# Feed-forward by seven products: product order, one more pair in part two's down projection, and left-side sums kept in DRAM

## The chip, the cores and the metric

The kernel runs on one core of one Trainium2 chip. The metric is the device time of one execution in microseconds (us); the median of several runs counts.

## What is computed

One layer of a decoder block on 256 tokens of width 2048, all in float32:

```
h = h + 1/2 * SwiGLU_a(RMSNorm(h))          # gate/up 2048 -> 2 x 5632, down 5632 -> 2048
h = h + mixer(RMSNorm(h))                    # one input projection, DeltaNet + stick-breaking, one output projection
h = h + 1/2 * SwiGLU_b(RMSNorm(h))
h = h + sigmoid(RMSNorm(h) @ W_pg) * (p @ W_pp)
out = RMSNorm(h)
swiglu(x) = (silu(x @ w_gate) * (x @ w_up)) @ w_down
```

The change touches the two SwiGLU feed-forwards alone.

## The kernel before

**Numbers.** Each float32 matrix is split into a high and a low part (fp32r), and a product takes three matmuls: high by high, high by low, low by high. Weights come from HBM as pairs: 256 rows by 512 columns, 512 KB, by `weight_pair` (L71 the load on SyncE's queue into one of four `raw` buffers, L74 the high part on ScalarE, L75 the low part on VectorE). A plain pair is 12 matmuls of 512 columns: 2 halves of the rows, 2 halves of the tokens, 3 matmuls each (L540 to L542 in the feed-forward). `next_weights` hands out the pairs in the order of one list and prepares up to two ahead.

**Groups.** A feed-forward (`ffn`) is a chain of groups of four PSUM banks (2 token halves by 2 column blocks). `PARTS` cuts the 11 blocks of the hidden width into part one (blocks 0 to 2), part two (3 to 6) and part three (7 to 10). Each part is one gate/up group ("gu") per block and then two down groups ("dn", column blocks 0 and 1, then 2 and 3) that contract over the part's blocks alone. A part of four blocks has eight pairs in its down projection, a part of three has six.

**Seven products.** Of each group the first `ns` pairs are not multiplied plainly. Over a pair, the two token halves, the two halves of the 256 rows and the two column blocks form a 2 by 2 by 2 block product, and the Winograd form needs seven products instead of eight: per pair 7 x 3 = 21 matmuls in place of 2 x 12 = 24. `NS` is 4 for gu groups and `NS_DOWN` is (2, 3, 3) for the down groups of the parts. Weight quarters of the `ns` pairs lie in four tiles R (L276, GpSimd's queue, `ns` x 256 KB each, named (0,0), (0,1), (1,1), (1,0)); `all_sums` makes the seven weight sides from them: VectorE sums (L304), accumulating DMAs on GpSimd's queue that add a quarter from HBM onto a tile (L311, `add_loaded`), and for each product a high part (L295, ScalarE) and a low part (L296, VectorE) in one of two buffers. The first three products take the running sums in (0,0), the fourth takes (0,1) after an accumulating DMA, the fifth takes (1,0) as loaded, the sixth (1,1), the seventh (0,0) after another accumulating DMA. `product` runs the matmuls (L339 to L341): first and second into banks c21 and c12, third and fourth into c21, fifth into c11, sixth into c12, seventh into c21. After the first two the result is copied to c11 and c22 (L344, ScalarE); after the third and the fourth c21 is copied out (L347, ScalarE) and subtracted from c12 or c22 (L349, VectorE). So the fourth product, which adds onto c21, waits for the copy of c21 after the third.

**Where the products stand.** A group's seven products are issued while the group before it does its plain pairs, one after each pair from the second or third pair on (`plan`). If the plain pairs run out, the rest follows the last one. The loads of R for the group after next are placed behind the fifth, sixth and seventh product and behind the next group's first plain pair, into the tiles in the order in which they come free (`loads`).

**Left sides.** Products one, five and seven take the left factor as it is; the other four take sums and differences of its quarters, made by `halves` in a lane beside the matmuls (L452 a sum, four L458, L460 high part on ScalarE, L461 low part on VectorE) into the tiles Sh and Sl. There is one pair of these tiles. They hold the normed input's sums ("gu"), then the hidden blocks' sums ("dn"), then the normed input's again: `halves("gu")` runs at the start of a feed-forward and again when the second down group of parts one and two begins (L518).

**The hidden blocks.** After a gu group `down_input` multiplies by the gate (L477), transposes on VectorE (L482), writes to DRAM (L488), reads back (L493, both on SyncE's queue for a part's last block) and splits (L499 ScalarE, L500 VectorE). The pairs of a part's last block come last in the first down group. `last` (L573) is the number of lane steps between the read and the split.

The order on each engine is set when the program is built: a scheduler takes the instructions in about the order of the source, but moves them past each other by what it expects to be ready; `keep_in_program_order` stops it from that for one instruction.

## Time and profile before

| | |
|---|---|
| median of 3 runs | 1952.89 us (1952.71 to 1953.48) |
| the profiled execution | 1953.25 us, of it 1951.5 us from the first to the last instruction |
| granted TensorE clock, mean | 0.998 |
| TensorE busy | 1932.7 us (99%), 8884 matmuls |
| VectorE busy | 1567.9 us (80%) |
| ScalarE busy | 1163.1 us (60%) |
| DMA | 475.06 MB, 243 GB/s over the span |

A share of the span is an average over stages. Matmuls are pipelined: each row shows some 389 ns, while the next one starts some 227 ns later, so time is read from start to start, and an idle time shown before a matmul leaves out the last one's tail (about 0.16 us).

### The profile page before, as it was taken

What the parts mean: (1) busy time and instruction counts of PE and PEld (TensorE: products, weight loads), DVE (VectorE), ACT (ScalarE), POOL (GpSimd) and SP (SyncE); (2) the same over time, 40 slices, a digit from 0 to 9 for tenths busy, and PEclk for the clock granted to TensorE, in tenths of its full rate; (3) what the DMA queues carried; (4) which work ended last, traced back from release to release, by engine and by line L of the source; (5) the groups of instructions that cost most, each with busy time, mean ns of one, the idle gap of its engine ahead of it and who ended that gap; (6) DMA issues with size and microseconds to landing.
All of it is one profiled execution on the core that took longest, in us unless ns stands there. A gap on an engine that the chain in (4) does not pass through costs nothing.

```text
span 1951.5 us, 24163 instructions
## 1 busy us (share of the span) xinstructions
PE 1932.7 (99%) x8884; PEld 1591.6 (82%) x8884; DVE 1567.9 (80%) x1679; ACT 1163.1 (60%) x1358; POOL 148.8 (8%) x226
## 2 busy tenths in 40 slices
PE   9999999999999999999999999999999999999997
PEld 7888888888888888878788888888888788887886
DVE  7889878997889766797856579889888987888965
ACT  6656666566665567664555456566565755656653
POOL 0010100000010000010100000010000100001000
PEclk9999999999999999999999999999999999999999
DMA  8778888788887765556565786888898987988864
GB/s 311 268 238 276 255 288 285 227 293 251 282 283 237 225 216 172 175 169 209 173 201 160 244 289 226 226 285 289 241 282 251 303 266 237 272 255 282 249 208 141
DMA packets 144184, 475.06 MB, mean 243 GB/s; under 512 B 19649, under 2 KB 47297, under 8 KB 129857
## 3 DMA queue, kind: packets, MB, share of 16 engines
q1 hardware_dynamic: 107200, 302.16, 44.4%
q0 software_dynamic: 25920, 160.44, 30.2%
q10 hardware_dynamic: 10944, 10.91, 1.7%
q8 instruction: 69, 1.13, 0.2%
q14 instruction: 51, 0.41, 0.1%
HBM read 451.44 MB, written 22.02 MB: 243 GB/s over the span
## 4 chain that ended last, share of the span: by engine, by line
PE 87%; DVE 6%; DMA 4%; issue 2%; ACT 1%; SPq 0%; POOL 0%; POOLq 0%; DVEq 0%; ACTq 0%
PE g L340 5%; PE d L541 5%; PE d L542 5%; PE g L339 5%; PE d L540 4%; PE g L341 4%; PE u L540 4%; PE u L542 4%; PE u L541 4%; PE g L541 4%; PE g L542 4%; PE pj L109 4%; PE pj L110 4%; PE pj L111 4%; PE g L540 4%
## 5 line engine op out<-in xcount | busy, mean ns | idle before, releaser
L74 ACT CAST whi<-raw 128x1024 fp32r<-128x1024 f32 (+1 forms) x489 | 512.1, 1050 | 427.1 <-PE pj L111 109.9
L75 DVE TENSOR_TENSOR wlo<-raw,whi 128x1024 fp32r<-128x1024 f32 (+1 forms) x489 | 592.0, 1217 | 166.1 <-ACT whi L74 163.8
L296 DVE TENSOR_TENSOR slo<-R,shi 128x2048 fp32r<-128x2048 f32 (+2 forms) x224 | 445.2, 1989 | 149.0 <-ACT shi L295 147.6
L295 ACT CAST shi<-R 128x2048 fp32r<-128x2048 f32 (+2 forms) x224 | 374.2, 1671 | 140.5 <-DVE R L304 62.1
L109 PE MATMUL pj<-whi,nTh 128*128 128x512 f32 x448 | 179.4, 401 | 0.0
L110 PE MATMUL pj<-wlo,nTh 128*128 128x512 f32 x448 | 175.3, 391 | 1.1 <-DVE wlo L75 1.1
L111 PE MATMUL pj<-whi,nTl 128*128 128x512 f32 x448 | 174.9, 390 | 0.0
L541 PE MATMUL d<-wlo,hTh 128*128 128x512 f32 x448 | 174.3, 389 | 0.0
L540 PE MATMUL d<-whi,hTh 128*128 128x512 f32 x448 | 174.2, 389 | 0.0
L542 PE MATMUL d<-whi,hTl 128*128 128x512 f32 x448 | 173.7, 389 | 0.0
L541 PE MATMUL g<-wlo,nTh 128*128 128x512 f32 x400 | 155.9, 390 | 0.4 <-DVE wlo L75 0.4
L541 PE MATMUL u<-wlo,nTh 128*128 128x512 f32 x400 | 155.7, 389 | 0.5 <-DVE wlo L75 0.5
L542 PE MATMUL g<-whi,nTl 128*128 128x512 f32 x400 | 155.8, 390 | 0.0
L542 PE MATMUL u<-whi,nTl 128*128 128x512 f32 x400 | 155.7, 389 | 0.0
L540 PE MATMUL g<-whi,nTh 128*128 128x512 f32 x400 | 155.4, 390 | 0.0
L540 PE MATMUL u<-whi,nTh 128*128 128x512 f32 x400 | 154.2, 389 | 0.2 <-ACT whi L74 0.2
L304 DVE TENSOR_TENSOR R<-R 128x2048 f32<-128x2048 f32 (+2 forms) x68 | 135.7, 1995 | 0.1
L110 PEld LDWEIGHTS pj<-wlo,nTh 128*128 128x128 f32 x448 | 84.2, 188 | 18.9 <-DVE wlo L75 2.7
L111 PEld LDWEIGHTS pj<-whi,nTl 128*128 128x128 f32 x448 | 84.1, 188 | 17.6
L542 PEld LDWEIGHTS d<-whi,hTl 128*128 128x128 f32 x448 | 84.1, 188 | 17.6
L541 PEld LDWEIGHTS d<-wlo,hTh 128*128 128x128 f32 x448 | 84.1, 188 | 17.6
L540 PEld LDWEIGHTS d<-whi,hTh 128*128 128x128 f32 x448 | 84.1, 188 | 17.4
(332 smaller groups left out, 3445.2 us busy)
## 6 DMA issues: line engine op xcount, KB each, us to landing
raw<-in_w_gu SPq DMA_DIRECT2D x199, 512.0 KB, 5.7
raw<-in_w_down SPq DMA_DIRECT2D x112, 512.0 KB, 6.5
raw<-in_w_in SPq DMA_DIRECT2D x112, 512.0 KB, 3.4
R<-in_w_gu2q POOLq DMA_DIRECT2D x54, 1024.0 KB, 8.6
R<-in_w_gu1q POOLq DMA_DIRECT2D x48, 1024.0 KB, 8.6
raw<-in_w_out SPq DMA_DIRECT2D x32, 512.0 KB, 4.2
tT<-scr SPq DMA_DIRECT2D x22, 512.0 KB, 5.1
R<-in_w_down11q POOLq DMA_DIRECT2D x12, 768.0 KB, 6.0
```

What stands on the lines that cost most here:

```text
L74: nc.scalar.copy(hi[:, j, :], raw[:, j, :])
L75: nc.vector.tensor_tensor(out=lo[:, j, :], in0=raw[:, j, :], in1=hi[:, j, :], op=ALU.subtract)
L109: nc.tensor.matmul(outs[t], xh[:, c], whi[:, j, :], start=st, stop=False)
L110: nc.tensor.matmul(outs[t], xh[:, c], wlo[:, j, :], start=False, stop=False)
L111: nc.tensor.matmul(outs[t], xl[:, c], whi[:, j, :], start=False, stop=sp)
L295: keep(nc.scalar.copy(hi, w))
L296: nc.vector.tensor_tensor(out=lo, in0=w, in1=hi, op=ALU.subtract)
L304: keep(nc.vector.tensor_tensor(out=self.raw[x], in0=self.raw[x], in1=self.raw[y], op=ALU.add))
L339: nc.tensor.matmul(out, xh, whi[:, g, :], start=st, stop=False, skip_group_check=True)
L540: nc.tensor.matmul(out, xh[:, c], whi[:, j, :], start=st, stop=False, skip_group_check=True)
L541: nc.tensor.matmul(out, xh[:, c], wlo[:, j, :], start=False, stop=False, skip_group_check=True)
L542: nc.tensor.matmul(out, xl[:, c], whi[:, j, :], start=False, stop=sp, skip_group_check=True)
```

## The change

Three things. The fifth product is put in front of the fourth (`SEVEN`), with its weight side, and the order in which the R tiles are taken over follows. The two down groups of part two take four pairs by seven products instead of three, so their plain pairs go from ten to eight each, and their left sides get a fourth pair. The sums of the normed input's left sides are written to DRAM once, sixteen lane steps after they are made, and read back into Sh and Sl in eight DMAs of 256 KB on SyncE's queue, at the second lane step of the second down group of parts one and two, instead of being computed again. The tiles Sh and Sl are laid out with the quarter outermost, and in part two `last` goes from 3 to 2.

```diff
@@ -28,7 +28,10 @@
 
 
 NS = 4
-NS_DOWN = tuple(3 if i1 - i0 == 4 else 2 for i0, i1 in PARTS)
+NS_DOWN = (2, 4, 3)
+
+
+SEVEN = (0, 1, 2, 4, 3, 5, 6)
 
 
 W_IN_ORDER = (2, 0, 4, 3, 1, 5, 8, 10, 12, 9, 11, 13, 6, 7)
@@ -278,7 +281,7 @@
         def loads(self, last=None):
 
 
-            free = [last.home[q] for q in ((0, 1), (1, 0), (1, 1), (0, 0))] if last else ["R0", "R1", "R2", "R3"]
+            free = [last.home[q] for q in ((1, 0), (0, 1), (1, 1), (0, 0))] if last else ["R0", "R1", "R2", "R3"]
             self.queue = nc.gpsimd if last else nc.sync
             use = (0, 0), (0, 1), (1, 1), (1, 0)
             self.home = dict(zip(use, free))
@@ -310,8 +313,8 @@
                     return add(x, y)
                 nc.gpsimd.dma_start(out=self.raw[x], in_=self.quarters[y[1]][y[0]], accum_op=ALU.add)
 
-            for i, q in enumerate(((0, 0), (0, 0), (0, 0), (0, 1), (1, 0), (1, 1), (0, 0))):
-                ws = halved(*q)
+            for i in SEVEN:
+                ws = halved(*((0, 0), (0, 0), (0, 0), (0, 1), (1, 0), (1, 1), (0, 0))[i])
                 if i == 0:
                     add((0, 0), (0, 1))
                     add_loaded((0, 1), (1, 1))
@@ -417,49 +420,69 @@
     order += [("pair", a["w_pg"][2][g]) for g in range(KD // 2)] + [("pair", a["w_pp"][2])]
     order.append(("pair", a["w_pp"][3]))
 
-    def halves(kind, his, los, ns, wait=0):
-
-
-        for _ in range(wait):
-            yield
-        fp = current[0]
-
-        sh = fp.tile([P, NS, 2, 2, P], F32R, tag="Sh", name="Sh")
-        sl = fp.tile([P, NS, 2, 2, P], F32R, tag="Sl", name="Sl")
+    def new_sides(kind, his, los):
+
+        sh, sl = [current[0].tile([P, 4, NS, P], F32R, tag=x, name=x) for x in ("Sh", "Sl")]
 
         def side(i, g):
             if i in (0, 4, 6):
                 k, t = 2 * (g % 2) + (i > 0), i // 6
                 c = slice(t * P, (t + 1) * P)
                 return his[g // 2][:, k, c], los[g // 2][:, k, c]
-            j, t = {1: (1, 1), 2: (0, 0), 3: (0, 1), 5: (1, 0)}[i]
-            return sh[:, g, j, t, :], sl[:, g, j, t, :]
+            jt = {1: 3, 2: 0, 3: 1, 5: 2}[i]
+            return sh[:, jt, g, :], sl[:, jt, g, :]
 
         sides[kind] = side
-
-        for g0 in range(0, ns, 2):
-            n = min(2, ns - g0)
-            hi, lo = his[g0 // 2], los[g0 // 2]
+        return sh, sl
+
+    def kept_sides(his, los, copy):
+
+        yield
+        both = new_sides("gu", his, los)
+        for jt in (3, 0, 1, 2):
+            for i in range(2):
+                nc.sync.dma_start(out=both[i][:, jt].bitcast(F32), in_=copy[:, i, jt])
+
+    def halves(kind, his, los, ns, wait=0, copy=None):
+
+
+        for _ in range(wait):
+            yield
+        fp = current[0]
+
+        both = new_sides(kind, his, los)
+        for g0, n in {1: ((0, 1),), 2: ((0, 2),), 3: ((0, 2), (2, 1)),
+                      4: ((0, 2), (2, 1), (3, 1)) if kind == "dn" else ((0, 2), (2, 2))}[ns]:
+            k0 = 2 * (g0 % 2)
+            hi, lo = (x[g0 // 2][:, k0:k0 + 2 * n] for x in (his, los))
             keep = lambda ins: ins
-            if g0 and n == 1:
+            if g0 >= 2 and n == 1:
 
                 keep = tc.keep_in_program_order
-                yield
+                if g0 == 2:
+                    yield
             if n == 2:
                 x = fp.tile([P, 2 * NB], F32, tag="sil", name="S")
             else:
                 x = act.tile([P, NB], F32, tag="nat", name="S", bufs=4)
-            keep(nc.vector.tensor_tensor(out=x, in0=hi[:, 0:2 * n].bitcast(F32).rearrange("p k x -> p (k x)"),
-                                         in1=lo[:, 0:2 * n].bitcast(F32).rearrange("p k x -> p (k x)"), op=ALU.add))
+            keep(nc.vector.tensor_tensor(out=x, in0=hi.bitcast(F32).rearrange("p k x -> p (k x)"),
+                                         in1=lo.bitcast(F32).rearrange("p k x -> p (k x)"), op=ALU.add))
             xv = x.rearrange("p (g j t y) -> p g j t y", g=n, j=2, t=2)
             a11, a12, a21, a22 = (xv[:, :, j, t, :] for t in range(2) for j in range(2))
             for o, y, z, op in ((a22, a21, a22, ALU.subtract), (a21, a11, a21, ALU.subtract),
                                 (a11, a22, a11, ALU.subtract), (a12, a11, a12, ALU.add)):
                 nc.vector.tensor_tensor(out=o, in0=y, in1=z, op=op)
-            sx = [y[:, g0:g0 + n].rearrange("p g j t y -> p (g j t y)") for y in (sh, sl)]
-            nc.scalar.copy(sx[0], x)
-            nc.vector.tensor_tensor(out=sx[1], in0=x, in1=sx[0], op=ALU.subtract)
-            yield
+            xs = x.rearrange("p (g c y) -> p c g y", g=n, c=4)
+            sx = [y[:, :, g0:g0 + n, :] for y in both]
+            nc.scalar.copy(sx[0], xs)
+            nc.vector.tensor_tensor(out=sx[1], in0=xs, in1=sx[0], op=ALU.subtract)
+            if g0 + n != 3 or ns == 3:
+                yield
+        if copy is not None:
+            for _ in range(16):
+                yield
+            for i in range(2):
+                nc.sync.dma_start(out=copy[:, i], in_=both[i].bitcast(F32))
 
     def ffn(n, nT, r, scale, next_norm, stat):
         xs = picker(*nT)
@@ -507,7 +530,8 @@
 
             nxt = None
             current[0] = fp
-            lanes.add(1, halves("gu", *nT, NS, 6 if late else 0))
+            copy = dr.tile([P, 2, 4, NS, P], F32, tag="sides", name="sides", bufs=2)
+            lanes.add(1, halves("gu", *nT, NS, 6 if late else 0, copy))
             for group, todo in ffn_plan[n]:
                 if group.kind == "behind":
                     break
@@ -515,7 +539,7 @@
                 i0 = PARTS[group.part][0]
 
                 if dn and group.nb and not group.last:
-                    lanes.add(1, halves("gu", *nT, NS))
+                    lanes.add(1, kept_sides(*nT, copy))
                 elif dn and group.nb and group.follower:
                     lanes.add(1, halves("behind", *nxt, NS_BEHIND, 4))
                 elif not dn and group.follower.kind == "dn":
@@ -526,7 +550,7 @@
                     group.new_banks()
                 for kind, one in todo:
                     if kind == "seventh":
-                        group.follower.product(one)
+                        group.follower.product(SEVEN[one])
                         continue
                     b, g = one
                     whi, wlo = next_weights()
@@ -570,7 +594,7 @@
                         hTl.append(tl)
                         i0, i1 = PARTS[group.part]
 
-                        last = (3 if i1 - i0 == 4 else 2) if len(hTh) == i1 else 0
+                        last = (6 - NS_DOWN[group.part] if i1 - i0 == 4 else 2) if len(hTh) == i1 else 0
                         gen = down_input(outs, sil, th, tl, last)
                         next(gen)
 
```

## Rows read from the trace of the kernel before

**Rows 1.** The page: part 1, busy us (share), instructions; part 6, KB, us to landing.
```profile
PE 1932.7 (99%) x8884; PEld 1591.6 (82%) x8884; DVE 1567.9 (80%) x1679; ACT 1163.1 (60%) x1358; POOL 148.8 (8%) x226
...
raw<-in_w_down SPq DMA_DIRECT2D x112, 512.0 KB, 6.5
```

**Rows 2.** Waits of PE: who waited for whom, us in total, times, longest.
```profile
PE d L339 <- ACT part L347: 2.7, 4, 0.7
```

**Rows 3.** Timeline, PE, first down group of part two: start us, us drawn, instruction.
```profile
405.06 0.39 PE L540 MATMUL d<-whi,hTh 128*128 128x512 f32 x1
...
410.95 0.39 PE L542 MATMUL d<-whi,hTl 128*128 128x512 f32 x1
```

**Rows 4.** Timeline, PE: starts of fourth products in down groups, and the matmul ahead.
```profile
160.36 0.39 PE L341 MATMUL d<-shi,Sl 128*128 128x512 f32 x1
161.43 0.50 PE L339 MATMUL d<-shi,Sh 128*128 128x512 f32 x1 [0.68 <-ACT part L347]
...
645.65 0.39 PE L542 MATMUL d<-whi,hTl 128*128 128x512 f32 x1
646.77 0.50 PE L339 MATMUL d<-shi,Sh 128*128 128x512 f32 x1 [0.73 <-ACT part L347]
...
1793.11 0.39 PE L542 MATMUL d<-whi,hTl 128*128 128x512 f32 x1
1793.58 0.50 PE L339 MATMUL d<-shi,Sh 128*128 128x512 f32 x1
```

**Rows 5.** Groups by line and form, VectorE's weight work: busy us, mean ns, idle before.
```profile
L75 DVE TENSOR_TENSOR wlo<-raw,whi 128x1024 fp32r<-128x1024 f32 x487 | 590.6, 1219 | 164.5 <-ACT whi L74 162.2 <-DMA tT<-scr 1.5
L296 DVE TENSOR_TENSOR slo<-R,shi 128x2048 fp32r<-128x2048 f32 x133 | 304.4, 2289 | 116.4 <-ACT shi L295 115.6 <-DMA raw<-in_w_gu 0.6
L296 DVE TENSOR_TENSOR slo<-R,shi 128x1536 fp32r<-128x1536 f32 x56 | 98.2, 1755 | 22.7 <-ACT shi L295 22.3
L304 DVE TENSOR_TENSOR R<-R 128x2048 f32<-128x2048 f32 x42 | 95.7, 2278 | 0.1
...
L304 DVE TENSOR_TENSOR R<-R 128x1536 f32<-128x1536 f32 x16 | 27.9, 1742 | 0.0
```

**Rows 6.** The same view, VectorE's left-side sums.
```profile
L458 DVE TENSOR_TENSOR S<-S 128x256 f32<-128x256 f32 x76 | 31.9, 420 | 0.9
...
L461 DVE TENSOR_TENSOR Sl<-S,Sh 128x1024 fp32r<-128x1024 f32 x19 | 23.2, 1222 | 3.9 <-ACT Sh L460 3.9
...
L452 DVE TENSOR_TENSOR S<-nTh,nTl 128x1024 f32<-128x1024 f32 x13 | 15.8, 1219 | 0.1
```

**Rows 7.** Timeline, part two's last gate/up group: ScalarE, then the fourth product's second matmul.
```profile
366.24 0.57 ACT L344 COPY d<-d 128x512 f32<-128x512 f32 x1 [1.98 <-PE d L341]
...
369.53 0.40 PE L542 MATMUL u<-whi,nTl 128*128 128x512 f32 x1
370.04 0.50 PE L340 MATMUL d<-slo,Sh 128*128 128x512 f32 x1
```

**Rows 8.** Timeline, part two's last hidden block: transposes, SyncE's read, low parts.
```profile
381.73 1.30 DVE L482 STREAM_TRANSPOSE tb<-sil 128x512 f32<-128x512 f32 x2
...
387.50 0.46 SPq L493 DMA_DIRECT2D tT<-scr  x1
...
398.94 1.28 DVE L500 TENSOR_TENSOR hTl<-tT,hTh 128x512 fp32r<-128x512 f32 x2
```

**Rows 9.** Windows: us; busy PE, PEld, DVE, ACT, POOL; clock; DMA share, GB/s.
```profile
370.00:400.00 30.00, 29.96 (x130) 24.16 (x131) 29.63 (x27) 20.72 (x23) 4.54 (x7) 1.00 0.86 268
```

**Rows 10.** DMA, 398 to 419 us: queue (q0 GpSimd's, q1 SyncE's), packets, MB, share.
```profile
q0 software_dynamic: 709, 4.91, 64.9%
q1 hardware_dynamic: 683, 2.52, 30.8%
```

**Rows 11.** Timeline, second down group of part two: a weight load and its low part's first matmul.
```profile
416.61 0.33 SPq L71 DMA_DIRECT2D raw<-in_w_down  x1
...
435.20 0.39 PE L541 MATMUL d<-wlo,hTh 128*128 128x512 f32 x1
```

## The prediction

> **What bounds the kernel now.** First the page: TensorE is busy 99% of the span, VectorE 80% [rows 1]. So every matmul that goes is worth its spacing, and all other work counts only where TensorE waits for it. The spacing comes from the timeline: 26 steps from 405.06 to 410.95 are 0.2265 us each [rows 3]; the drawn 0.39 us is no price. Then the waits of TensorE: the largest is a down product's first matmul waiting for ScalarE's copy of c21, 2.7 us in four waits [rows 2]. In the timeline these are the starts of fourth products right behind the third, which both use c21: 160.36 to 161.43 is 1.07 us where 0.2265 would do, 0.84 lost; 0.89 at 646.77; 0.24 at 1793.58, too short for the list of waits [rows 4]. The other two of the four waits are taken as the mean of the rest: drawn idle leaves out 0.16 each, so 2.7 + 4 x 0.16 + 0.24 = 3.6 us in five stalls, one each in parts one and three of both feed-forwards and one in part two of the second. Last, VectorE by windows: 29.63 of 30 us while part two's first down group runs [rows 9]. There a longer VectorE chain can reach TensorE.
>
> **Fewer matmuls.** Part two has two down groups in each of two feed-forwards. In each, one pair goes from 24 plain matmuls to 21: 4 x 3 x 0.2265 = 2.7 us off the bound engine. The Trainium skill ("TensorE: Matmul & The Clock Gate", "Wait — 56ns, not 53.3ns?") has 215.7 ns for a warm matmul of 512 columns; by that it would be 2.6 us. The row is 5% longer and decides.
>
> **Fifth product before the fourth.** The fifth goes into c11 with an unchanged left factor, so nothing of the third product holds it, and its weight quarter is used as loaded, while the fourth waits for an accumulating DMA. Between the third and the fourth then lie a whole product and mostly a pair. The two stalls of part three (0.89 and 0.24) and that of part two (0.8) have no other late input beside them: I count them whole, 1.9. In part one the matmuls behind the stall need the part's last hidden block, so some of 2 x 0.84 is a wait in another name; I take 1.4. Together 3.3 of 3.6. Bounds: 1.1 (part three alone) to 3.6. The fourth's copy must now be out before the seventh adds onto c21, with the sixth between: at least 6 x 0.2265 = 1.4 us (two pairs) against the 1.07 us that the copy took with nothing between, so nothing. The R tiles are taken over in the new order of release; the quarter (1,0), loaded last, is wanted one product earlier, and a product with its pair is 18 matmuls or more, 4.1 us. It is loaded a whole group ahead; nothing.
>
> **VectorE's sums, over both feed-forwards.** Out: eight computations of sums of 1024 columns, each 1.219 + 4 x 0.420 + 1.222 = 4.1 us [rows 6], 33.0. Eight plain pairs less, 8 x 1.219 = 9.8 out. In: 28 weight low parts of 2048 columns instead of 1536, 28 x (2.289 - 1.755) = 15.0; eight weight sums, 8 x (2.278 - 1.742) = 4.3 [rows 5]; left sides of a fourth pair, half of 4.1 us at least, some 2.5 with four short instructions, twice, 5. Net 18.5 us less, worth nothing directly: no wait of TensorE names these sums in the second down groups, where the 33.0 go. But the additions come earlier, in the last gate/up group and the first down group of part two, where VectorE is full.
>
> **New cost in part two, twice.** (a) The second product of the first down group needs the fourth pair's left sides too, some 2.5 us later. ScalarE already sits 1.98 us behind it, because the copy of the second product stands ahead of the next weight side in its queue; the high part, VectorE's low part and TensorE follow, and that ends in a stall of 0.51 - 0.23 = 0.28 us now [rows 7]. Cover: a plain down pair that could be taken first, 12 x 0.2265 = 2.7 us. (b) Only four plain pairs instead of six come before those of the last hidden block. That block is ready at 398.94 + 1.28 = 400.2; TensorE comes to it at 405.06 [rows 3, 8]: 4.8 us spare. Ahead of it go away two pairs (24 matmuls) and two products (18), and come 21 matmuls of the first down group's own fourth pair and 9 of the three products left: net 12, 2.7 us. Spare 2.1. Five low parts ahead of the transposes cost VectorE 5 x 0.53 = 2.7 us more, the fourth pair's sides up to 2.5: the block is 2.7 to 5.2 us later, 0.6 to 3.1 short. Cover: the fifth product, which in its new place may be moved ahead, 2.7 us. With the cover used I take 0.8 for (a) and (b) together, 1.6 for both feed-forwards; without it up to 3.5 each. Lower bound: the present stall goes, -0.3 each. What the taken-out sums would have delayed behind it (one of 1.2 us stood in VectorE's queue before the low parts) is the reason that it may be below nothing.
>
> **Sides through DRAM.** Written once: 2.1 MB in two DMAs per feed-forward. Read twice: eight DMAs on SyncE's queue, which must wait for the sixth product of the last down group to leave Sh and Sl; behind them stand the weight loads of the next pairs, and ScalarE's casts wait for those. No row shows such a read. Bounds: all queues together moved 4.91 + 2.52 MB in 21 us, 354 GB/s, and at that 2.1 MB takes 5.9 us; at SyncE's own 2.52 MB in 21 us it takes 17.5 [rows 10]. A load issued at 416.61 serves a matmul at 435.20 [rows 11]; less 6.5 us of loading [rows 1], 1.22 for the low part and no more than that for the cast, about 9.7 us are spare. So from nothing to 17.5 - 9.7 = 7.8 us for each of four reads. I take nothing: the loads of R end while the read begins, so its share should rise towards the first end. The writes I take at nothing too (no reader for tens of us), bounded by 1 us each.
>
> **Sum.** The profiled execution took 1953.25 us, 0.36 above the median. 1953.25 - 2.7 - 3.3 + 1.6 = 1948.9; at the median 1948.5.
>
> **Rivals.** *The hidden block comes too late.* The 18.5 us are saved after the place where VectorE is full, and the last block's chain and the second product take the freed time: 2 to 7 us more over both feed-forwards than I count, 1949 to 1954, centre 1951.5. For it: 29.63 of 30 us [rows 9], and a spare that the sum uses up. Against: the cover of 2.7 us at each place. *The stalls only move.* The scheduler sets the order, and a different matmul may meet the same copy or a late block; then little but the 12 matmuls is left: 1952.9 - 2.7, 1950.2 or a little more. For it: in part one the stalled matmuls had already been moved ahead of a plain pair. *Slower: the side reads hold up weight loads.* At four places the loads behind 2.1 MB land late. It decides from the point where SyncE's queue gets less than 2.1 MB in 9.7 us, 216 GB/s. Price: at SyncE's share so far 4 x 7.8 = 31 us; with the loads of R ending during the read, perhaps 3 us each, 12 in all: 1960.5. The Trainium skill ("DMA: Bandwidth & Descriptors", "Queues, rings and completion order") says that a DMA engine goes round its queues packet by packet, so two busy queues should get half each; the row shows 2 to 1 against SyncE. By half of 354 GB/s a read takes 11.9 us, 2.2 over the spare, 9 us for the four, and the kernel takes 1957.5.
>
> **How the numbers follow.** About 0.2% of 1952.89, 3.9 us, is what a measurement of this kernel tells from no change: faster is below 1949.0, slower above 1956.8. The forecast has 0.50 (its own range 1946 to 1949), the late block 0.25, the stalls that move 0.13, the reads 0.12. Faster 0.50, same 0.38, slower 0.12. The range goes from 1946.0, with all stalls and the low bounds, to 1955.0, through the second and third case; the reads and what lies below, about 0.15, stay out.
>
> **What would show it.** 8872 matmuls. No wait of a down product for the copy of c21. In part two, the gap at the first plain pair of the last hidden block, and at the second down product: under 1 us each would bear me out, more is the first rival. Around each read: weight casts waiting for DMA and idle TensorE would be the slower case; casts that wait while TensorE does not would show the delay inside the spare. Computed sums (L452 on nTh and nTl) fall from 13 to 5. Wrong would be above all a static order that puts the late instructions in front.

## The result, and the profile after

The changed kernel is slower: 1958.55 us (median of 6 runs, 1957.88 to 1963.25) against 1952.74 us of the kernel before beside it, a ratio of 1.0037 with a 95% interval of 1.0027 to 1.0047. That is 5.8 us more, where I had forecast 4.4 less. The profiled execution took 1957.89 us, its span 1956.2 us.

First the page of the changed kernel, part 1, then the waits of TensorE over the whole span (who waited for whom, us in total, times, longest):

```profile
PE 1928.8 (99%) x8872; PEld 1589.7 (81%) x8872; DVE 1557.3 (80%) x1635; ACT 1161.1 (59%) x1344; POOL 148.4 (8%) x226
```
```profile
PE d L342 <- ACT shi L298: 4.0, 4, 1.1
PE g L564 <- ACT whi L77: 3.2, 3, 2.1
PE d L343 <- DVE slo L299: 3.0, 4, 1.3
PE u L565 <- DVE wlo L78: 3.0, 3, 1.3
```

The 12 matmuls are gone, 8884 to 8872 [rows 1]. The wait for the copy of c21, the largest of before [rows 2], is gone as well. Three groups of waits for weight parts, nearly all in part two, and one for weights at the starts of the two feed-forwards have taken its place, 13.2 us in 14 waits.

Where they lie is in TensorE's timeline of part two of the first feed-forward (start us, us drawn, instruction, and in brackets what the idle time ended with). Steps are 0.2265 us [rows 3], so what a start is later than that is lost:

```profile
357.30 0.50 PE L565 MATMUL u<-wlo,nTh 128*128 128x512 f32 x1 [1.28 <-DVE wlo L78]
...
373.95 0.40 PE L566 MATMUL u<-whi,nTl 128*128 128x512 f32 x1
375.43 0.50 PE L342 MATMUL d<-shi,Sh 128*128 128x512 f32 x1 [1.08 <-ACT shi L298]
...
381.25 0.39 PE L565 MATMUL d<-wlo,hTh 128*128 128x512 f32 x1
382.93 0.50 PE L343 MATMUL d<-slo,Sh 128*128 128x512 f32 x1 [1.29 <-DVE slo L299]
...
404.39 0.39 PE L342 MATMUL d<-shi,Sh 128*128 128x512 f32 x1
405.69 0.50 PE L342 MATMUL d<-shi,hTh 128*128 128x512 f32 x1 [0.91 <-ACT shi L298]
```

The stall at 375.43 costs 375.43 - 373.95 - 0.23 = 1.25 us, the one at 382.93 costs 1.45, the one at 405.69 costs 1.07. Ahead of them stands one of 1.44 us, at 357.30, at a plain up pair that waits for its low part. Together 5.2 us, and part two of the second feed-forward has the same four (1506.57, 1524.68, 1532.18, 1554.93).

The queues of VectorE and ScalarE in the last gate/up group show what they are made of (timeline, first VectorE, then ScalarE):

```profile
350.04 2.29 DVE L299 TENSOR_TENSOR slo<-R,shi 128x2048 fp32r<-128x2048 f32 x1
352.24 0.42 DVE L474 TENSOR_TENSOR S<-S 128x256 f32<-128x256 f32 x1
352.57 2.29 DVE L307 TENSOR_TENSOR R<-R 128x2048 f32<-128x2048 f32 x1
354.77 1.34 DVE L474 TENSOR_TENSOR S<-S 128x256 f32<-128x256 f32 x3
356.03 1.22 DVE L78 TENSOR_TENSOR wlo<-raw,whi 128x1024 fp32r<-128x1024 f32 x1
...
364.31 0.69 DVE L478 TENSOR_TENSOR Sl<-S,Sh 128x512 fp32r<-128x512 f32 x1
364.91 0.69 DVE L468 TENSOR_TENSOR S<-hTh,hTl 128x512 f32<-128x512 f32 x1
...
369.35 0.69 DVE L478 TENSOR_TENSOR Sl<-S,Sh 128x512 fp32r<-128x512 f32 x1
373.13 2.29 DVE L299 TENSOR_TENSOR slo<-R,shi 128x2048 fp32r<-128x2048 f32 x1 [3.09 <-ACT shi L298]
```
```profile
370.70 0.57 ACT L347 COPY d<-d 128x512 f32<-128x512 f32 x1 [2.00 <-PE d L344]
371.18 1.91 ACT L298 CAST shi<-R 128x2048 fp32r<-128x2048 f32 x1
372.99 0.59 ACT L350 COPY part<-d 128x512 f32<-128x512 f32 x1
373.46 1.91 ACT L298 CAST shi<-R 128x2048 fp32r<-128x2048 f32 x1
```

The fourth pair's sides run from 364.91 to 370.04, since weight low parts stand between them. The second product can end only behind them. Its copy of c22 therefore comes at 370.70, where the kernel before had it at 366.24 [rows 7], and it waits 2.00 us at the head of ScalarE's queue. The high parts of the next two products stand behind it (371.18 and 373.46), VectorE waits 3.09 us for the first, and TensorE at 375.43 for the second. At 357.30 it is the plain low part of 356.03, behind a weight sum of 2.29 us and four side sums.

The window that I had read for the bound of VectorE [rows 9] has in the changed kernel (us; busy PE, PEld, DVE, ACT, POOL; clock; DMA share, GB/s):

```profile
370.00:400.00 30.00, 27.62 (x119) 21.72 (x118) 26.25 (x21) 19.22 (x17) 3.08 (x5) 1.00 0.83 281
```

VectorE is busy 26.25 us there, less than the 29.63 of before, while TensorE lost 2.3 us of busy time: all three engines wait for each other in turn. The drop itself depends on the window, since this one holds VectorE's wait of 3.09 us. Over 340 to 410 us, which holds all four stalls, VectorE is about as busy as before while TensorE loses 4.4 us (first the kernel before, then the changed one):

```profile
340.00:410.00 70.00, 69.88 (x305) 56.48 (x305) 65.02 (x66) 42.68 (x44) 7.94 (x12) 1.00 0.83 262
```
```profile
340.00:410.00 70.00, 65.44 (x281) 51.63 (x280) 64.58 (x62) 40.81 (x40) 6.29 (x9) 1.00 0.80 241
```

A busy share doesn't show such a chain.

### The profile page after: what moved, and what is told of

Read it like the earlier page. It is cut to its first block, busy times and chain, and to the rows that moved or that the text cites. A ratio compares the mean times of both kernels' runs of the same rounds, so it can differ in the third digit from the quotient of the medians.

```text
span 1956.2 us, 24075 instructions
## 1 busy us (share of the span) xinstructions
PE 1928.8 (99%) x8872; PEld 1589.7 (81%) x8872; DVE 1557.3 (80%) x1635; ACT 1161.1 (59%) x1344; POOL 148.4 (8%) x226
## 4 chain that ended last, share of the span: by engine, by line
PE 87%; DVE 8%; DMA 2%; issue 2%; ACT 2%; POOL 0%; SPq 0%; POOLq 0%; DVEq 0%; ACTq 0%
PE d L566 5%; PE d L564 5%; PE d L565 5%; PE g L342 4%; PE g L344 4%; PE g L343 4%; PE u L565 4%; PE u L566 4%; PE u L564 4%; PE pj L112 4%; PE pj L113 4%; PE pj L114 4%; PE g L565 4%; PE g L566 4%; PE g L564 4%; PE d L343 2%
## 5 line engine op out<-in xcount | busy, mean ns | idle before, releaser
L77 ACT CAST whi<-raw 128x1024 fp32r<-128x1024 f32 (+1 forms) x481 | 503.7, 1050 | 431.1 <-PE pj L114 106.3
L78 DVE TENSOR_TENSOR wlo<-raw,whi 128x1024 fp32r<-128x1024 f32 (+1 forms) x481 | 582.6, 1217 | 164.2 <-ACT whi L77 163.4
L299 DVE TENSOR_TENSOR slo<-R,shi 128x2048 fp32r<-128x2048 f32 (+2 forms) x224 | 460.0, 2056 | 154.1 <-ACT shi L298 152.0
L298 ACT CAST shi<-R 128x2048 fp32r<-128x2048 f32 (+2 forms) x224 | 385.7, 1724 | 130.9 <-DVE R L307 58.3
L564 PE MATMUL d<-whi,hTh 128*128 128x512 f32 x416 | 162.0, 390 | 0.0
L565 PE MATMUL d<-wlo,hTh 128*128 128x512 f32 x416 | 161.9, 389 | 0.0
L566 PE MATMUL d<-whi,hTl 128*128 128x512 f32 x416 | 161.6, 389 | 0.0
L114 PEld LDWEIGHTS pj<-whi,nTl 128*128 128x128 f32 x448 | 84.1, 188 | 17.5
L112 PEld LDWEIGHTS pj<-whi,nTh 128*128 128x128 f32 x448 | 84.2, 188 | 16.7
L564 PEld LDWEIGHTS d<-whi,hTh 128*128 128x128 f32 x416 | 78.1, 188 | 17.0 <-ACT hTh L522 1.0
L565 PEld LDWEIGHTS u<-wlo,nTh 128*128 128x128 f32 x400 | 75.1, 188 | 20.4 <-DVE wlo L78 5.0
```

What stands on the lines that cost most here:

```text
L77: nc.scalar.copy(hi[:, j, :], raw[:, j, :])
L78: nc.vector.tensor_tensor(out=lo[:, j, :], in0=raw[:, j, :], in1=hi[:, j, :], op=ALU.subtract)
L112: nc.tensor.matmul(outs[t], xh[:, c], whi[:, j, :], start=st, stop=False)
L114: nc.tensor.matmul(outs[t], xl[:, c], whi[:, j, :], start=False, stop=sp)
L298: keep(nc.scalar.copy(hi, w))
L299: nc.vector.tensor_tensor(out=lo, in0=w, in1=hi, op=ALU.subtract)
```

## The experiments

Medians are compared with runs of the kernel before on the same chip (1951.4 to 1952.4 us). The stretches are each from one profiled execution. "Part two" is the time from the first gate/up matmul of part two to that of part three in TensorE's timeline; in the changed kernel these two rows are

```profile
219.39 0.39 PE L564 MATMUL g<-whi,nTh 128*128 128x512 f32 x1
...
470.91 0.39 PE L564 MATMUL g<-whi,nTh 128*128 128x512 f32 x1
```

so 251.52 us. "Start" is likewise the time up to part two of the first feed-forward, from that feed-forward's first gate/up matmul (5.83 here), 213.56 us.

| run | time, us | against before, us | ratio (95%) | part two, us, first / second feed-forward |
|---|---|---|---|---|
| before | 1952.74 | | | 247.69 / 248.60 |
| changed kernel | 1958.55 | +5.8 | 1.0037 (1.0027 to 1.0047) | 251.52 / 251.52 |
| swap alone | 1948.82 | -3.6 | 0.9982 (0.9973 to 0.9991) | 247.69 / 247.70 |
| swap, DRAM | 1949.32 | -3.1 | 0.9986 (0.9976 to 0.9995) | 247.37 / 247.59 |
| swap, four pairs | 1957.74 | +5.3 | 1.0028 (1.0016 to 1.0039) | 254.03 / 254.01 |
| third pair's sides twice | 1951.25 | -1.1 | 0.9996 (0.9986 to 1.0005) | 248.21 / 248.36 |
| four pairs, second group only | 1949.12 | -2.6 | 0.9988 (0.9979 to 0.9997) | 248.10 / 248.12 |
| sides computed, not read | 1950.32 | -1.4 | 0.9995 (0.9986 to 1.0004) | 247.97 / 247.94 |
| no sums, first down group | 1949.80 | -1.9 | 0.9990 (0.9981 to 0.9999) | 247.46 / 247.43 |
| fifth product second | 1953.66 | +1.9 | 1.0010 (1.0001 to 1.0019) | 249.10 / 249.10 |
| second group only, later | 1950.66 | -1.1 | 0.9993 (0.9985 to 1.0002) | 249.04 / 248.61 |
| swap, DRAM, writes kept in program order | 1949.42 | -2.3 | 0.9989 (0.9980 to 0.9998) | 247.40 / 247.63 |
| second group only, later, DRAM | 1951.93 | +0.1 | 1.0001 (0.9992 to 1.0009) | 248.42 / 248.45 |
| swap again | 1948.21 | -3.6 | 0.9982 (0.9973 to 0.9991) | 247.76 / 247.74 |
| swap, DRAM in the second feed-forward only | 1947.85 | -3.6 | 0.9982 (0.9973 to 0.9991) | 247.77 / 247.41 |
| no sums, both down groups | 1947.40 | -4.0 | 0.9979 (0.9970 to 0.9988) | 246.37 / 246.33 |

With the swap alone part two takes 247.69; six matmuls less would make it 247.69 - 6 x 0.2265 = 246.33. The changed kernel is 5.2 us above that in each feed-forward, as much as the four stalls together. The match is good to some 0.7 us only: the 246.33 still hold two small waits of the swap alone, 0.31 and 0.38 us, that the changed kernel doesn't have.

**The parts of the change one by one.** The swap alone:

```diff
...
-            for i, q in enumerate(((0, 0), (0, 0), (0, 0), (0, 1), (1, 0), (1, 1), (0, 0))):
+            for i in SEVEN:      # (0, 1, 2, 4, 3, 5, 6), and the order of release with it
```

> The kernel before with the fifth product in front of the fourth and nothing else. If the order does what the prediction says, the five waits for the copy of c21 (3.6 us from start to start) go and the time falls by 3 to 3.6 us, to about 1949.3. If the new order itself puts late matmuls in front (the kernel with all three changes shows a matmul of a moved product waiting at 375.4 and 405.7), part two loses 2 us or more per feed-forward here too and the time is 1951 or above.

Measured 1948.82, 3.6 us less. Run again beside others: 1948.21 against 1951.78, again 3.6.

> The swap alone once more, beside the three others on one chip, so that they are compared with it directly: 1948.8, 3.6 below the kernel before.

The changed kernel with three pairs in part two, that is swap and DRAM copy:

```diff
-NS_DOWN = (2, 4, 3)
+NS_DOWN = (2, 3, 3)
```

> New order and left sides through DRAM, but three pairs in part two's down groups. If the fourth pair makes the loss, part two is as fast as in the kernel before (about 247.7 us in the first feed-forward) and only the start of the first feed-forward loses, some 1.5 us, because the writes stand ahead of the first R loads: 1950 to 1951.5. If the reads of the sides hold up weight loads, part two and the kernel stay slow: 1955 or above.

Measured 1949.32: the copy costs about 0.5 us, less than the intervals tell apart, and nothing in part two. The reads do hold up loads, and a cast waits for them; the timeline of ScalarE in this run:

```profile
432.31 1.05 ACT L77 CAST whi<-raw 128x1024 fp32r<-128x1024 f32 x1 [6.68 <-DMA raw<-in_w_down]
```

But no matmul waits there. The changed kernel without the DRAM copy:

```diff
...
-                    lanes.add(1, kept_sides(*nT, copy))
+                    lanes.add(1, halves("gu", *nT, NS))
```

> New order and four pairs, left sides computed again as before (no DRAM). If the fourth pair makes the loss through a full VectorE, part two stays at 251 us or above and the time is 1957 to 1960, no better than with all three, since VectorE also has the 33 us of sums back. If the DRAM part made the loss, part two falls to about 247 us and the time to 1948 to 1950.

Measured 1957.74, 8.9 above the swap alone. So the fourth pair is the loss, with or without DRAM. In the profiled executions part two is 2.5 us shorter with the copy (251.52 against 254.03), but only 0.8 of it is VectorE's relief: without the copy the stall near 405 is 1.89 us instead of 1.07. Another 1.6 us are TensorE's clock. Behind that stall the granted clock fell to the lower of its two levels, 1.2 GHz, and eight matmuls from 406.91 on stand 0.43 us apart (windows, columns as above, first this run, then the changed kernel):

```profile
407.00:410.00 3.00, 3.00 (x9) 2.35 (x8) 2.00 (x3) 1.84 (x4) 0.57 (x1) 0.50 0.92 137
```
```profile
407.00:410.00 3.00, 3.00 (x15) 2.47 (x14) 2.76 (x4) 2.48 (x4) 0.56 (x1) 1.00 0.93 142
```

The second feed-forward has the same. This execution took 1960.93 us, 3.2 above the median of the run, so the two falls of the clock are probably not in its usual executions, and by the medians the copy takes off nothing (+5.3 without it, +5.8 with it).

**Is it the fourth pair's left sides?** The changed kernel with the fourth pair's left-side sums of hidden blocks left out, the third pair's read in their place:

```diff
+            g = min(g, 2) if kind == "dn" else g
...
-                      4: ((0, 2), (2, 1), (3, 1)) if kind == "dn" else ((0, 2), (2, 2))}[ns]:
+                      4: ((0, 2), (2, 1)) if kind == "dn" else ((0, 2), (2, 2))}[ns]:
```

> All three changes, but the fourth pair's left-side sums of the hidden blocks are left out (the third pair's stand in for them, so six VectorE operations and a cast per feed-forward are not done and the result is another). If the second product's wait for these sums starts the loss (term a of the prediction), 2.5 us of VectorE work less ahead of it should give back 2 to 4 us in each feed-forward: 1951 to 1954. If the loss comes from the longer weight low parts and sums (2048 columns instead of 1536), it stays at 1957 to 1958.

Measured 1951.25: 7 us of the loss are back. This run leaves out both the work on the sums and the reading of them.

From here two theories stand against each other. "Wait": a product waits for sides that come late, and what stands behind its copy waits with it. "Load": VectorE has too much to do there, whoever reads the results. The next run leaves VectorE all its work and takes away only the reading:

```diff
+            if i not in (0, 4, 6) and kind == "dn":
+                g = min(g, 2)
```

> The changed kernel, but the fourth pair's left-side sums of hidden blocks, which are all still computed on VectorE and ScalarE, are read by no product: the products read the third pair's in their place (the output is therefore another). Theory 'wait': as with those sums left out, 1951.3, since no product waits for them any more. Theory 'load': as the changed kernel, 1957.5 to 1958.6, since VectorE does the same work. In between, each has its share.

Measured 1950.32, and part two 247.97, no slower than with the sums left out (248.21): the wait counts, and not VectorE's time for these sums. That time is 0.69 + 1.27 + 0.69 = 2.65 us in the changed kernel (364.91, 366.65 and 369.35); where the expectations put it at 4.4 us, or at as much as two weight sums (4.6), that is too much. The order was not quite kept: in this run the fourth pair's cast and low part, 0.62 and 0.69 us, come behind the next weight part. Only two of the four stalls are left, one of 0.84 at 402.47 and the plain pair's, unchanged:

```profile
357.63 0.50 PE L567 MATMUL u<-wlo,nTh 128*128 128x512 f32 x1 [1.28 <-DVE wlo L78]
```

Next the other side: the reading stays, and VectorE's two sums of weight quarters of the first down group are left out.

```diff
             def add(x, y):
+                if (self.kind, self.part, self.nb) == ("dn", 1, 0):
+                    return
```

> The changed kernel without VectorE's two sums of weight quarters of part two's first down group (two of 2.28 us in each feed-forward left out, the products use the quarters as they were loaded, so the output is another). Theory 'wait': only the stall of a plain pair that stood behind the first of these sums goes, 1.2 us in each feed-forward: 1956.2. Theory 'load': 4.6 us of VectorE less in each feed-forward ahead of the fourth pair's sides, which is as much as those sides themselves, so most of the loss goes: 1951 to 1953.

Measured 1949.80, far below what "wait" alone had given (1956.2) and below the range of "load". So neither theory holds alone. The sides are late because of what stands ahead of them on VectorE, and their lateness costs because a product waits for them; take either away and most of the loss goes. VectorE's timeline of this run has the fourth pair's low part at

```profile
367.84 0.69 DVE L480 TENSOR_TENSOR Sl<-S,Sh 128x512 fp32r<-128x512 f32 x1 [0.69 <-ACT Sh L479]
```

Part two starts at 221.46 in this run, so this is 146.4 us into it, where the changed kernel has it at 369.35 - 219.39 = 150.0. With 3.6 us earlier sides the stall of 375.43 isn't there, the plain pair's isn't either, and the one of 382.93 is down from 1.45 to 0.82 us. The stall near 405 stayed (0.87 us). In the changed kernel the high part that it waits for stood behind a weight sum of the second down group on VectorE, at 399.02, and behind the copy that comes before it on ScalarE; the late hidden block was the other suspect (VectorE's and ScalarE's timelines of the changed kernel):

```profile
399.02 2.29 DVE L307 TENSOR_TENSOR R<-R 128x2048 f32<-128x2048 f32 x1
```
```profile
403.74 1.90 ACT L298 CAST shi<-R 128x2048 fp32r<-128x2048 f32 x1
406.17 1.15 ACT L522 CAST hTh<-tT 128x512 fp32r<-128x512 f32 x2 [0.53 <-DMA tT<-scr]
```

> The changed kernel without VectorE's sums of weight quarters in both down groups of part two (four of 2.28 us in each feed-forward left out, so the output is another). One stall of about 0.9 us in each feed-forward was left when only the first group's sums were out: the second group's second product waited for a high part, behind a sum on VectorE. If VectorE's queue is what makes that high part late, it goes too: 1949.8 - 1.8 = 1948.0. If the part's last hidden block, which ScalarE and VectorE take at the same time, is what makes it late: 1949.8 again.

The condition above was widened to both down groups of part two. Measured 1947.40, and part two takes 246.37 and 246.33 us, the 246.33 worked out above. What is left of TensorE's waits for slo in part two is one of 0.8 us:

```profile
378.75 0.50 PE L345 MATMUL d<-slo,Sh 128*128 128x512 f32 x1 [0.66 <-DVE slo L299]
```

The swap alone has waits of this kind too, 0.31 and 0.38. So it was the sum, not the hidden block, whose split stands behind that high part anyway (406.17 above). With four sums of 2.28 us less the fourth pair costs nothing more in part two, its sides included. No run leaves these sums out of the swap alone, so what they cost there isn't known.

**The wait with nothing left out.** The changed kernel with the fifth product in second place, in part two's first down group alone. Its sides need no sums, so the second product comes later. The order in which its quarters are loaded follows.

```diff
...
+            self.early = (kind, part, nb) == ("dn", 1, 0)
+            self.seven = (0, 4, 1, 2, 3, 5, 6) if self.early else SEVEN
...
```

> The changed kernel with another order of the products in part two's first down group alone: first, fifth, second, third, fourth, sixth, seventh. The fifth takes left sides that are used unchanged, so the second, the first to want the fourth pair's sums, comes a product and mostly a pair later (24 and some matmuls of 0.2265 us, over 5 us); nothing is left out. The third and the fourth stand side by side again, which cost up to 0.9 us in a part. Theory 'wait' (the second product waits for the fourth pair's sides, which VectorE's load makes late): the two stalls of 1.25 and 1.45 us in each feed-forward go, at most 0.9 comes back: 1957.9 - 2 x (2.7 to 1.8) and what followed on them, 1952 to 1954.5. If the stalls come from VectorE's work itself: as the changed kernel, 1957.5 to 1958.6.

Measured 1953.66, 4 us better than the changed kernel by the difference to before, inside the range of "wait". Part two is 2.4 us shorter. It still has stalls of 1.25, 0.69 and 1.51 us. The first is again a plain pair's low part behind a weight sum, at 365.48, some 7 us further on than in the changed kernel.

**The fourth pair in the second down group only** (the first keeps three; nothing through DRAM):

```diff
-NS_DOWN = (2, 4, 3)
+NS_DOWN = ((2, 2), (3, 4), (3, 3))     # per down group; the last side AFTER = 4 steps later
...
```

> The swap alone, and four pairs by seven products only in the second down group of part two (the first keeps three; every side is computed, nothing goes through DRAM). 8878 matmuls, 6 fewer than with the swap alone: 6 x 0.2265 = 1.4 us. Theory 'wait' (what costs is that the second product of the first down group waits for the fourth pair's left sides, with the next weight's high part behind it on ScalarE): in the second group the fourth pair's sides are made many pairs ahead, so nothing waits, and the time is 1948.8 - 1.4 = 1947.4. Theory 'load' (what costs is VectorE's volume while it is full): the fourth pair's sums, 4.4 us, and longer low parts, 7 x 0.53 = 3.7 us, now fall into the stretch in which VectorE was busy 29.63 of 30 us, and the time is 1951 to 1955.

Measured 1949.12, between the theories. One stall is left in each feed-forward, 1.4 us, at a plain pair whose low part stood on VectorE behind the side sums, two transposes and a weight sum:

```profile
386.57 0.61 PE L564 MATMUL d<-whi,hTh 128*128 128x512 f32 x2
388.44 0.50 PE L565 MATMUL d<-wlo,hTh 128*128 128x512 f32 x1 [1.25 <-DVE wlo L79]
```

So I moved the side sums three pairs later (AFTER = 7).

> The swap, and four pairs only in part two's second down group, as in the second-group run; there one stall was left in each feed-forward, 1.4 us at a plain pair whose low part stood on VectorE behind the fourth pair's sums. Here these sums come three pairs later. Theory 'wait': that stall goes and nothing new waits: 1949.1 - 2.8 = 1946.3, or 1947.4 if a part of it comes back as a late hidden block. Theory 'load': VectorE has the same work in the same stretch, so the stall only moves: 1949.1.

Measured 1950.66, worse. The plain pair's stall went, but now the second product waits for the sides themselves:

```profile
400.09 0.61 ACT L478 CAST Sh<-S 128x512 fp32r<-128x512 f32 x1
```
```profile
398.77 0.39 PE L344 MATMUL d<-slo,Sh 128*128 128x512 f32 x1
400.75 0.50 PE L343 MATMUL d<-shi,Sh 128*128 128x512 f32 x1 [1.59 <-ACT Sh L478]
```

At four pairs the sums hold up a low part, at seven they come too late; in this stretch "load" is right in that the stall only moved. Whether a place between is free of both wasn't tried.

**What the DRAM copy costs.** The 0.5 us had to be the writes or the reads. The start takes 212.4 to 213.2 us in the five runs above that have the swap and write no sides, and 213.6 to 215.6 us in the nine that write them in the first feed-forward. The two longest of these (swap with DRAM, 215.1, and no sums in the first down group, 215.6) also have TensorE's clock at its lower level for about 3 us behind the wait shown below (granted 0.57 from 67 to 71 us); the other seven reach 214.8. In the changed kernel the writes stand on SyncE's queue ahead of the first loads of quarters (timeline of SP):

```profile
39.93 0.43 SPq L485 DMA_DIRECT2D sides<-Sh  x1
40.40 0.42 SPq L485 DMA_DIRECT2D sides<-Sl  x1
42.27 3.05 SPq L74 DMA_DIRECT2D raw<-in_w_gu  x2
45.37 6.64 SPq L279 DMA_DIRECT2D R<-in_w_gu1q  x4
```

I tried to have them later, once by keeping their place in the program and once by six more steps, the latter on the kernel of the run before.

```diff
-                nc.sync.dma_start(out=copy[:, i], in_=both[i].bitcast(F32))
+                tc.keep_in_program_order(nc.sync.dma_start(out=copy[:, i], in_=both[i].bitcast(F32)))
```

> Swap and sides in DRAM, three pairs in part two, but the two DMAs that write the sides keep their place in the program, behind the first loads of weight quarters, where the scheduler had moved them ahead of these. If the 0.5 us that DRAM cost over the swap alone are the writes ahead of the first quarters (TensorE waited 1.6 us there for a weight's high part), they go: 1948.8 or a little below. If they are the reads, or chance: 1949.3 again.

```diff
-            for _ in range(16):
+            for _ in range(22 if wait else 16):
```

> As the run before it, and with the left sides kept in DRAM, written six pairs later in the first feed-forward. VectorE has then 4.1 us less in each second down group. If what is left is VectorE's load: 0.5 to 1 us below the run before it. If the DRAM copy costs at the start as it did beside the swap alone: 0.5 us above it.

Measured 1949.42 (2.3 less than before) and 1951.93 (0.1 more). Neither moved the writes of the first feed-forward: they went out at 40.53 and 40.58, still ahead of the quarters at 45.97 and 45.80. So these two runs don't say what a later write is worth; the second says that the copy costs 1.3 us there. The last run does the copy in the second feed-forward alone:

```diff
-            copy = dr.tile([P, 2, 4, NS, P], F32, tag="sides", name="sides", bufs=2)
+            copy = None if n == "1" else dr.tile([P, 2, 4, NS, P], F32, tag="sides", name="sides", bufs=2)
...
```

> Swap and three pairs in part two, with the left sides kept in DRAM in the second feed-forward alone; the first computes them each time as the kernel before. If what DRAM costs is the two writes of the first feed-forward, which go out while the DMA engines are busy with the first weights and quarters: part one of the first feed-forward takes 213.2 us as with the swap alone (not 214.6 as with both copies), and the second feed-forward keeps its small gain: 1947.9 to 1948.8. If the reads cost, the second feed-forward shows it as well: 1949.3.

Measured 1947.85 against 1951.40, a ratio of 0.9982 (0.9973 to 0.9991). The start takes 212.39 us, as without a copy. The window shows why, first of the changed kernel, then of this run (columns as above):

```profile
36.00:66.00 30.00, 28.37 (x126) 23.15 (x124) 20.38 (x20) 15.77 (x18) 0.71 (x1) 1.00 0.97 373
```
```profile
36.00:66.00 30.00, 29.66 (x130) 23.90 (x128) 22.31 (x20) 18.01 (x21) 0.71 (x1) 1.00 0.86 318
```

The DMA engines have no room there: with the writes their share is 0.97, and the 1.6 MB more that are moved (55 GB/s in 30 us) push back the quarters and the pairs behind them: the pair behind the quarters lands at 65.27 where this run has it at 61.07. ScalarE waits for it, and TensorE for ScalarE (the changed kernel):

```profile
65.37 1.04 ACT L77 CAST whi<-raw 128x1024 fp32r<-128x1024 f32 x1 [0.81 <-DMA raw<-in_w_gu]
```
```profile
66.47 0.74 PE L564 MATMUL g<-whi,nTh 128*128 128x512 f32 x2 [2.10 <-ACT whi L77]
```

So the cost of the copy is in its writes in the first feed-forward, not in the reads, which the second feed-forward of this run has without loss. This kernel and the swap alone are the best of those that compute everything, both 3.6 us ahead of the kernel before; their difference is below what can be measured.

## Why the prediction was wrong

**Fewer matmuls: right.** 8872, and in the run without weight sums, which has nearly no stalls, part two is 246.33 to 246.37 us, 1.36 under the swap alone.

**Fifth before fourth: right.** Forecast 3.3, measured 3.6 twice with the swap alone. Not one wait for the copy of c21 is left. My doubt about part one was not needed.

**The step that failed is (a) of "New cost in part two", with the cover that it shared with (b).** I took 0.8 us for each feed-forward for (a) and (b) together, at most 3.5; it is 5.2, 10.4 in all. The place was right: the second product waits for the fourth pair's sides, its copy at the head of ScalarE's queue, the next high part behind it. Three things in its price were wrong. *The size of the delay:* I let the sides add 2.5 us, by their own work; the copy came 370.70 - 366.24 = 4.5 us later (4.0 counted from the start of part two), since the other low parts of VectorE stand between them. *What was on the chain:* I had counted the longer low parts and weight sums, 0.53 us each, as VectorE's time only. They are links of the chain, and so is the longer high part, which I didn't count at all: 1.91 us at 371.18 instead of 1.48 at 366.72, right behind the copy of [rows 7] (row of ScalarE below). Two stalls, the plain pair's at 357.30 and that near 405, come from a weight sum of 2.28 us ahead of a low or a high part, and both went when these sums were left out. *The cover:* I set 2.7 us of another pair against each delay. The order on TensorE is fixed when the kernel is built, and the pairs that could have filled the gaps stood behind the waiting matmuls.

```profile
366.72 1.48 ACT L295 CAST shi<-R 128x1536 fp32r<-128x1536 f32 x1
```

**Part (b), the late hidden block: its delay was more than I had, its cost nothing.** The transposes come at 388.19 instead of 381.73 [rows 8], 6.5 us later (6.0 counted from the start of part two), and the low parts end at 409.2 instead of 400.2 (8.5 later, counted likewise); I had 2.7 to 5.2. TensorE comes to their pairs at 408.58 without a gap. The timeline of VectorE and of SyncE, which answer to [rows 8]:

```profile
388.19 1.30 DVE L505 STREAM_TRANSPOSE tb<-sil 128x512 f32<-128x512 f32 x2
...
407.88 1.29 DVE L523 TENSOR_TENSOR hTl<-tT,hTh 128x512 fp32r<-128x512 f32 x2
```
```profile
396.81 0.51 SPq L516 DMA_DIRECT2D tT<-scr  x1
```

The stalls further ahead had given it time. With only two of them left, in the run with the sides unread, it came in time as well, so what the block would cost without any stall isn't shown. My rival of the late block named VectorE's chain in the right stretch, but with the wrong last link, and with 2 to 7 us over both feed-forwards where part two lost 10.4 - 1.6 = 8.8 more than I counted.

**The sides through DRAM: the reads rightly at nothing, the writes not.** That VectorE is relieved came true (computed sums fall from 13 to 5, [rows 6] against the row below, from the groups by line and form), and it helped a little more than the "nothing directly" that I gave it: the stall near 405, which I hadn't foreseen, is 0.8 us shorter with the copy than without in each feed-forward.

```profile
L468 DVE TENSOR_TENSOR S<-nTh,nTl 128x1024 f32<-128x1024 f32 x5 | 6.1, 1223 | 0.1
```

The slower case that I had feared, reads that hold up weight loads, isn't what made the kernel slower: there is no wait of TensorE at any of the four reads. That its 1957.5 lies near the measured time is luck. Its sizes were not bad: the first read of part two was issued at 424.64, and the eight had landed at 436.43, 11.8 us, and 17.1 us in the run with swap and DRAM, within my 5.9 to 17.5 (19.3 and 20.2 in the run with four pairs in the second group only, later, and DRAM). The spare time behind them was larger than my 9.7 us. The writes, which I had at nothing with no reader near, cost a wait of 2.1 us at the start, because I looked for who reads them and not for who shares the DMA engines with them.

**With the sizes measured** the sum is 1953.25 - 2.7 - 3.6 + 10.4 for part two + 0.7 for the start (213.56 in this execution against 212.8, the mean of the six without a copy in the first feed-forward; other waits there are shorter) = 1958.05, where 1957.89 was measured.

## What to carry to other kernels

Price a delay along the chain on which it lies (side, product, copy, high part, low part, product), with every link at its new size, and not by the busy share of an engine: here VectorE was no busier than before and TensorE waited more. Work covers a wait only if it stands ahead of the waiting instruction in its engine's fixed order. And of a write that nobody waits for, ask what else is in the DMA engines at that time.

## What the runs showed of the hardware

Sharing between two DMA queues was not the 2 to 1 against SyncE of [rows 10] everywhere. While the sides were read in the changed kernel (424.6 to 436.4 us) SyncE's queue moved the larger part (queue, packets, MB, share):

```profile
q1 hardware_dynamic: 1416, 3.07, 73.1%
q0 software_dynamic: 158, 1.12, 23.4%
```

The Trainium skill ("DMA: Bandwidth & Descriptors", "Queues, rings and completion order") says that a DMA engine takes its queues in turn, packet by packet. From that I had put each of two busy queues at half of the bytes, an estimate of 11.9 us for a read. The read took 11.8 us, but not by halves: the rows have 3.07 against 1.12 MB. With three pairs in part two the same read took 17.1 us, near the 17.5 of SyncE's share so far, and again SyncE's queue moved more, 3.61 against 2.66 MB (411.4 to 428.5 us). So neither agreement bears its rule out, and whether GpSimd's queue had work all the while isn't shown: neither is a bound to build on.
